# HGRN2 decays by doubling products, and other rotations for a dilated attention, in a two-layer trunk on one core

## The chip, the cores and the metric

The kernel runs on one core of a Trainium2 chip. TensorE (PE) multiplies matrices into PSUM; VectorE (DVE), ScalarE (ACT) and GpSimd (POOL) do the elementwise work, and SyncE (SP) issues every DMA here, in one queue and in order. GpSimd works on SBUF tiles only here. The metric is the time of one execution in microseconds, as the median of several; lower is better.

## The reference

A trunk of two residual layers for 1024 tokens of width 1024, all float32. Layer 0 has a gated DeltaNet and a short convolution as its mixer, layer 1 has HGRN2 and a dilated window attention; a SwiGLU FFN follows each. The change is in layer 1's mixer. What it computes, cut:

```python
hq, hf, hi, hg, sq, sk, sv = split_cols(h @ w_in, CD_SPLITS)
f_gate = lb + (1.0 - lb) * sigmoid(hf)              # 4 heads of 128
k_in   = (1.0 - lb) * sigmoid(-hf)                  # = 1 - f_gate
# HGRN2: S_t = diag(f_t) S_{t-1} + k_t v_t^T,  o_t = S_t^T q_t,  q = silu(hq), v = hi
o_c = rms_norm(o, norm_g) * sigmoid(hg)
# attention: patterns (window, dilation) = (128, 1), (512, 4), (2048, 16), 4 heads of 128 each
sq, sk = rope(sq, pos), rope(sk, pos)
outs, lses = dilated_window_attention(...)          # per pattern, causal
o_d = sum over patterns of outs * softmax(lses over patterns)
return concatenate([o_c, o_d]) @ w_out
```

## The kernel before

Activations are feature-major: 128 features in the partitions, tokens along the row, in two halves of 512 tokens (`HT`). A product in float32 is three matmuls of high and low parts (`mm3`, lines 126 to 128), so a projection of 128 columns for a half is 8 x 3 = 24 matmuls of 512 columns. `wload` (L109) loads a block of weights into a ring (two tiles for raw data, four for the split parts) and splits it with ScalarE (L102) and VectorE (L103). PSUM has 2 banks for `psg`, 3 for `psu`, 3 for `psm`.

Layer 1 before its mixer makes queries, keys, HGRN queries and forget gates in the class `Pairs`: two column blocks at a time, by seven products of half the size, 84 matmuls of 512 columns for a pair where 96 would be plain. `HEADS` lists its sixteen pairs: ("k", p, h) is query and key of pattern p (0, 1, 2 for dilation 1, 4, 16) and head h; ("f", h) is forget gate and query of an HGRN head. The results go to DRAM: `pairs.qk` unrotated, and `pairs.bkq` with b, k and q of a head, where `forget` computes the gate f, its logarithm and a running sum b over 128 tokens by scans.

`mixer_cd` then holds all other work of the mixer. Its outer sequence is dense: value projections of HGRN (`hgrn_v`) and of the three patterns (`swa_v`, in the order 1, 2, 0), then the gates (`hgrn_gates`). Every few matmuls it calls `tick`, which advances two generators by rates: `chain`, the HGRN units, and `local`, the attention with its combine (L2071 to L2080). So the program's text interleaves them; the order on each engine, PE too, is then chosen by the scheduler, by its own estimates.

An HGRN unit is one head and one half, eight in all (`hgrn`). For seven block sizes bs = 1, 2, ..., 64, `decayed` makes a tile m: for every pair of neighbouring blocks it takes b minus its value at the boundary (L1712, L1714), the exponential on ScalarE (L1715), and multiplies by k in the earlier (L1716) and q in the later block (L1720). Products of m with itself in 32x32 blocks on PE (L1728, L1759, L1783) give the masked scores, which are gathered in `attn`. Then k times its decay is transposed (L1790), the states are made (L1798, L1809), and the output of the unit is normalised: sum of squares (L1823, L1824), the power -1/2 `rr` on GpSimd (L1826), a diagonal matrix of it on VectorE (L1828), and a product of the output with that matrix (L1834), which transposes and scales at once.

Attention loads a head's query and key, twice: once as they are and once (`rs`) with the two halves of the features exchanged. GpSimd multiplies these by the tables of sine (L1935) and cosine (L1939), VectorE adds (L1944).

## Time and profile before

| what | us |
| --- | --- |
| three runs | 2648.23, 2653.04, 2654.51; median 2653.04 |
| the profiled execution | 2653.24 |
| its span, the profile's own scale | 2651.4 |
| mean granted clock of TensorE | 0.988 |
| layer 0's mixer | until about 480 |
| layer 0's FFN | 480 to 1141 |
| the pairs | 1141 to 1461 |
| layer 1's mixer | 1461 to 1925 |
| output projection, FFN, final norm | 1925 to 2651 |

The page of the profile gives busy time by engine, the span in 40 slices of 66.3 us, the chain of work that ended last, and groups of instructions by line. Views of the trace give the same by stretch of time (windows), by what an engine waited for (waits), and instruction by instruction (timelines). L1712 means line 1712 of the kernel before. In a row of a group, "x56 | 31.2, 565" is 56 instructions, 31.2 us in all and 565 ns on average, and behind the next bar stands the idle time of the engine ahead of them with what ended it. A stretch where the granted clock is 0.50 has TensorE at half speed.

### The profile page before, as it was taken

The numbers are of one execution on the slowest core, as the hardware profiler recorded it, in microseconds if no ns is written. First come the engines' busy times: TensorE is split into PE (matmuls) and PEld (weight loads), VectorE is DVE, ScalarE is ACT, GpSimd is POOL, SyncE is SP. The second block draws the span as 40 slices with busy tenths as digits, with TensorE's granted clock in tenths as the row PEclk, the third lists the DMA queues.
The fourth block names the chain that finished last, engine by engine and source line by source line (L and its number), as shares of the span: only waits on it lengthen the run. The fifth ranks groups of instructions, "written<-read, shape, count | busy, mean of one in ns | idle before, by whom it ended". The sixth has DMA issues, their size and how long they took to land.

```text
span 2651.4 us, 37677 instructions
## 1 busy us (share of the span) xinstructions
PE 2569.4 (97%) x14163; PEld 2136.8 (81%) x14163; DVE 1731.2 (65%) x2809; ACT 1023.3 (39%) x1719; POOL 677.7 (26%) x552
## 2 busy tenths in 40 slices
PE   8999999999999999999999898998799999999998
PEld 6888888888888888878888777876688888888887
DVE  7887776585655665576665665579767655656554
ACT  4432123343333344434444344444444333334442
POOL 1110111333333200133232313345023433331001
PEclk9999999999999999999999899998999999999999
DMA  4424347325556687623333636876562555658763
GB/s 140 136 97 164 108 146 228 130 86 184 179 201 207 223 295 261 193 88 139 120 122 128 183 124 172 184 208 185 172 228 69 170 171 184 218 198 288 265 192 119
DMA packets 277606, 457.79 MB, mean 173 GB/s; under 512 B 49424, under 2 KB 133936, under 8 KB 276912
## 3 DMA queue, kind: packets, MB, share of 16 engines
q1 hardware_dynamic: 277424, 455.39, 53.6%
q8 instruction: 111, 1.82, 0.3%
q14 instruction: 71, 0.58, 0.1%
HBM read 315.23 MB, written 140.07 MB: 172 GB/s over the span
## 4 chain that ended last, share of the span: by engine, by line
PE 84%; DVE 9%; DMA 3%; issue 2%; POOL 1%; ACT 1%; SPq 0%; DVEq 0%; POOLq 0%; ACTq 0%
PE psu L126 16%; PE psu L127 15%; PE psu L128 15%; PE psg L126 6%; PE psg L128 6%; PE psg L127 6%; PE psm L128 4%; PE psm L126 4%; PE psm L127 4%; DMA raw<-in_dram 1%; DVE h L223 1%; DVE h L592 1%; DMA cm<-scr_o 1%; PE psm L199 1%; DVE w L289 1%
## 5 line engine op out<-in xcount | busy, mean ns | idle before, releaser
L103 DVE TENSOR_TENSOR w<-raw,w 128x1024 fp32r<-128x1024 f32 (+1 forms) x323 | 383.9, 1190 | 158.2 <-ACT w L102 157.6
L102 ACT CAST w<-raw 128x1024 fp32r<-128x1024 f32 (+1 forms) x323 | 309.3, 959 | 287.7 <-PE psu L128 137.6
L126 PE MATMUL psu<-hnh,w 128*128 128x512 f32 x848 | 339.9, 401 | 13.0 <-ACT w L102 7.0
L127 PE MATMUL psu<-hnl,w 128*128 128x512 f32 x848 | 332.9, 393 | 0.8 <-DVE hnl L2186 0.8
L128 PE MATMUL psu<-hnh,w 128*128 128x512 f32 x848 | 332.9, 393 | 0.0
L126 PEld LDWEIGHTS psu<-hnh,w 128*128 128x128 f32 x848 | 161.0, 190 | 46.6 <-ACT w L102 7.0
L302 POOL TENSOR_TENSOR ws<-raw 128x512 f32<-128x512 f32 x54 | 82.0, 1519 | 428.6 <-DMA raw<-in_dram 230.7
L128 PEld LDWEIGHTS psu<-hnh,w 128*128 128x128 f32 x848 | 160.4, 189 | 34.8 <-DVE w L103 0.8
L127 PEld LDWEIGHTS psu<-hnl,w 128*128 128x128 f32 x848 | 160.8, 190 | 33.4 <-DVE hnl L2186 1.3
L187 POOL TENSOR_TENSOR acc<-acc,sq 128x512 f32<-128x512 f32 x48 | 69.9, 1456 | 439.4 <-ACT sq L183 439.4
L103 DVE TENSOR_TENSOR w<-ws,w 128x1024 fp32r<-128x1024 f32 x51 | 65.8, 1290 | 114.0 <-ACT w L102 114.0
L103 DVE TENSOR_TENSOR hidq<-hr,hidq 128x1024 fp32r<-128x1024 f32 x72 | 82.1, 1141 | 73.6 <-ACT hidq L102 73.1
L102 ACT CAST hidq<-hr 128x1024 fp32r<-128x1024 f32 x72 | 70.2, 980 | 100.3 <-DMA hr<-ts 58.1
L308 POOL TENSOR_TENSOR raw<-raw,ws 128x512 f32<-128x512 f32 x51 | 68.0, 1334 | 158.0 <-DVE w L103 156.7
L126 PE MATMUL psm<-hidq,w 128*128 128x512 f32 (+1 forms) x275 | 106.0, 385 | 0.0
L127 PE MATMUL psm<-hidq,w 128*128 128x512 f32 (+1 forms) x275 | 105.8, 385 | 0.0
L128 PE MATMUL psm<-hidq,w 128*128 128x512 f32 (+1 forms) x275 | 105.8, 385 | 0.0
L393 POOL TENSOR_TENSOR hid<-hid,c 128x512 f32<-128x512 f32 x44 | 62.8, 1427 | 125.6 <-ACT hid L392 125.3
L126 PE MATMUL psu<-t4h,w 128*128 128x512 f32 x240 | 93.7, 391 | 0.6 <-ACT c L372 0.6
L127 PE MATMUL psu<-t4l,w 128*128 128x512 f32 x240 | 93.4, 389 | 0.0
L128 PE MATMUL psu<-t4h,w 128*128 128x512 f32 x240 | 93.4, 389 | 0.0
L126 PE MATMUL psu<-t3h,w 128*128 128x512 f32 x240 | 93.4, 389 | 0.0
(491 smaller groups left out, 6774.6 us busy)
## 6 DMA issues: line engine op xcount, KB each, us to landing
raw<-in_dram SPq DMA_DIRECT2D x227, 512.0 KB, 4.0
sd<-in_dram SPq DMA_DIRECT2D x44, 512.0 KB, 3.9
hid<-hid SPq DMA_DIRECT2D x88, 256.0 KB, 2.8
sd<-sd SPq DMA_DIRECT2D x44, 512.0 KB, 3.3
hr<-ts SPq DMA_DIRECT2D x40, 512.0 KB, 4.7
raw<-sd SPq DMA_DIRECT2D x40, 512.0 KB, 4.0
hd<-h SPq DMA_DIRECT2D x48, 256.0 KB, 3.9
h<-hd SPq DMA_DIRECT2D x48, 256.0 KB, 5.6
```

Of the source, the lines that this page charges most:

```text
L102: S.copy(hi, src)
L103: eng.tensor_tensor(lo, src, hi.bitcast(F32), op=SUB)
L126: T.matmul(o, lh, rh, start=first and i == 0, stop=False, **kw)
L127: T.matmul(o, lh, rl, start=False, stop=False, **kw)
L128: T.matmul(o, ll, rh, start=False, stop=last and i == n - 1, **kw)
L187: (eng or G).tensor_tensor(a, a, q, op=ADD)
L199: T.matmul(st[:, j:j + 1], x[:, j * P:(j + 1) * P], onesn, start=i + j == 0, stop=i == 1, skip_group_check=True)
L223: V.scalar_tensor_tensor(h, h, vec[:, row + k:row + k + 1], pb, op0=MULT, op1=MULT)
L289: later(lambda: V.tensor_tensor(u[:, 1, c], src[:, c], u[:, 0, c].bitcast(F32), op=SUB))
L302: G.tensor_tensor(s[:, HT:], b[:, :HT], b[:, HT:], op=ADD)
L308: G.tensor_tensor(a[:, HT:], a[:, HT:], s[:, :HT], op=SUB)
L393: G.tensor_tensor(h, h, self.c22.pop(f), op=MULT)
```

## The change

Decays without logarithms: `forget` stores f itself; the scans and the logarithm go. A unit copies k into kd, and q times f into qd. `level` copies the halves of kd and qd that its products need into m (ScalarE), and then multiplies, in place, kd in the earlier block of each pair by the later block's total decay and qd in the later block by the earlier one's. The totals d of the next level, half as many, are the products of neighbours (`dd`, from 256 down to 4 elements). After the seventh level kd, qd and d are what the states need, so the exponentials at the end go too. f, kk and q have one buffer instead of two. HGRN's values go through DRAM (`scr_h`).

The unit's end: ScalarE sums the squares, the output is scaled from PSUM by `rr` at the start of the next unit (`ending[0]`), and transposed by PE after the next unit's first products (`ending[1]`).

Rotations: pattern 1's queries and keys leave the pairs (`HEADS` has twelve entries) and are plain projections in the mixer (`swa_qk`), rotated by VectorE straight from PSUM. Patterns 2 and 0 are rotated by `turns`, a third generator: 32 items (pattern, head, query or key, half), each loaded, rotated by three GpSimd operations, and stored to DRAM (`final`), from which `Attend` loads it. The combine uses scaled copies on ScalarE and 128x128 multiply-adds on VectorE.

Order: PE follows the text inside `mixer_cd` (`manual_schedule`), the other engines still the scheduler. `tick` advances three generators. At the mixer's end the first three banks of the output projection are begun (`leading`).

```diff
-        HEADS = (("k", 0, 0), ("k", 0, 1), ("k", 0, 2), ("f", 0), ("k", 1, 0), ("k", 1, 1), ("f", 1), ("k", 1, 2),
-                 ("k", 1, 3), ("f", 2), ("k", 2, 0), ("k", 2, 1), ("f", 3), ("k", 2, 2), ("k", 2, 3), ("k", 0, 3))
+        HEADS = (("k", 0, 0), ("k", 0, 1), ("k", 0, 2), ("f", 0), ("k", 2, 0), ("f", 1), ("k", 2, 1), ("f", 2),
+                 ("k", 2, 2), ("f", 3), ("k", 2, 3), ("k", 0, 3))
 
...
-            for c, r in zip(cs, rs):
-                S.activation(r, c, AF.Ln, scale=self.omlb[:, h:h + 1], bias=self.lb[:, h:h + 1])
-            yield
-            for half, (c, r) in enumerate(zip(cs, rs)):
-                for j in range(4):
-                    t = slice(j * P, (j + 1) * P)
-                    V.tensor_tensor_scan(c[:, t], onec[:, 0:1].to_broadcast([P, P]), r[:, t], 0.0, op0=MULT, op1=ADD)
+                S.activation(c, c, AF.Identity, scale=om, bias=lb)
                 dma(self.bkq[h, half][0], c)
                 yield
 
...
-                    raws[u] = [hl(n, bufs=2) for n in ("b", "kk", "q")]
+                    raws[u] = [hl(n) for n in ("f", "kk", "q")]
...
-            def hgrn(h, half, states):
...
-                    m = hl("m", bufs=3)
-                    mb = v4(m)
-                    ref = bb[:, :, 0, bs - 1:bs].to_broadcast([P, n, bs])
-                    V.tensor_tensor(mb[:, :, 1, :], bb[:, :, 1, :], ref, op=SUB)
-                    if bs > 1:
-                        V.tensor_tensor(mb[:, :, 0, :], ref, bb[:, :, 0, :], op=SUB)
-                        S.activation(m, m, AF.Exp)
-                        V.tensor_tensor(mb[:, :, 0, :], mb[:, :, 0, :], kb[:, :, 0, :], op=MULT)
-                    else:
-                        S.activation(mb[:, :, 1, :], mb[:, :, 1, :], AF.Exp)
-                        S.copy(mb[:, :, 0, :], kb[:, :, 0, :])
-                    V.tensor_tensor(mb[:, :, 1, :], mb[:, :, 1, :], qb[:, :, 1, :], op=MULT)
...
+            def level(bs, k, q, d, dd, at):
+
+                n = HT // (2 * bs)
+
+                def v4(ap):
+                    return ap.rearrange("p (n a j) -> p n a j", a=2, j=bs)
+                m, kb, qb, d3 = hl("m", bufs=4), v4(k), v4(q), d.rearrange("p (n a) -> p n a", a=2)
+                S.copy(v4(m)[:, :, 0, :], kb[:, :, 0, :])
+                S.copy(v4(m)[:, :, 1, :], qb[:, :, 1, :])
+                for x, i in ((kb, 0), (qb, 1)):
+                    V.tensor_tensor(x[:, :, i, :], x[:, :, i, :], d3[:, :, 1 - i:2 - i].to_broadcast([P, n, bs]), op=MULT)
+                nd = dd[:, at:at + n]
+                V.tensor_tensor(nd, d3[:, :, 0], d3[:, :, 1], op=MULT)
+                return m, nd, at + n
...
+            def hgrn(u, states, ending):
+                h, half = divmod(u, 2)
+                f, kk, q = raws.pop(u)
+                kd, qd, dd = hl("kd"), hl("qd", bufs=2), hl("dd")
+                state = [f, 0]
+
+                def next_level(bs):
+                    m, state[0], state[1] = level(bs, kd, qd, state[0], dd, state[1])
                     return m
...
-                ms = [decayed(1), decayed(2)]
+                ending[0]()
+                S.copy(kd, kk)
+                V.tensor_tensor(qd, q, f, op=MULT)
+                ms = [next_level(1), next_level(2)]
+                yield
+                ms.append(next_level(4))
+                yield
+                od = psg()
+                blocks(od[:, 0:P], kk, q)
+                for i in range(3):
+                    blocks(od[:, (i + 1) * P:(i + 2) * P], ms[i], ms[i])
+                ending[1]()
+                ac = hl("ac", (4, 32))
+                V.tensor_tensor(ac, c4(od[:, 0:P]), dia32[:, None, :].to_broadcast([P, 4, 32]), op=MULT)
+                for i in range(3):
+                    take(i, od[:, (i + 1) * P:(i + 2) * P])
+                ask(u + 1)
+                ms = [next_level(8), next_level(16)]
...
+                oq, ss, rr = hl("e4", (4, P), 3), hl("ss", (4,), 2), hl("rr", (4,), 2)
+                for c in range(4):
+                    S.activation(oq[:, c, :], po[:, c * P:(c + 1) * P], AF.Square, accum_out=ss[:, c:c + 1])
+                V.tensor_scalar(ss, ss, 1.0 / P, 4 * EPS, op0=MULT, op1=ADD)
+                with tc.high_priority(offset=300):
+                    G.tensor_tensor(rr, ss, mhalf[:, 0:4], op=ALU.pow)
...
+                def scaled():
+                    V.tensor_tensor(os_, c4(po), rr[:, :, None].to_broadcast([P, 4, P]), op=MULT)
+
+                def end():
+                    o = psg()
+                    for c in range(4):
+                        T.transpose(o[:, c * P:(c + 1) * P], os_[:, c, :], ident)
+                    go = hl("e4", (4, P), 3)
+                    S.activation(go, c4(o), AF.Copy, scale=hgg)
+                    dma(scr_g[half, h].rearrange("p (c t) -> p c t", c=4), go)
+                    done_c[0] = u + 1
                 yield
...
-                    T.matmul(o[:, c * P:(c + 1) * P], os_[:, c, :], dg[:, c, :], start=True, stop=True)
-                go = hl("e4", (4, P), 3)
-                V.tensor_scalar(go, c4(o), vec[:, R_HGG:R_HGG + 1], 0.5, op0=MULT, op1=MULT)
...
+            def leading(tick):
...
+                ws[2] = wload(("cdo", 2), ("cdo", 3))
+                for d, bank in ((0, psg), (1, psg), (2, psu)):
+                    o = banks[d] = bank()
+                    for ks in ((0, 1), (2, 3), (4, 5)):
+                        proj(wk(ws[d // 2 * 2], d % 2), qs, ks, o, first=ks[0] == 0, last=False)
+                        tick(0.5)
...
+            turn12 = tl("turn12", (2, 320))
+            dma(turn12, c_rope[:, :, T_LEN:])
+            final = {(p, h): dr.tile([2, P, 2, HT], F32, name=f"fin{p}{h}") for p in (2, 0) for h in range(4)}
...
+            def swa_qk(h, tick):
+
+                w = wload(("cd", 20 + h), ("cd", 32 + h))
+                qk = [tl("q", (2, HT), 2), tl("k", (2, HT), 2)]
+                for half in range(NH):
+                    for i, z in enumerate(qk):
+                        o = proj(wk(w, i), hn[half], range(KH), last=False)
+                        tick(1)
+                        proj(wk(w, i), hn[half], range(KH, KT), o, first=False)
+                        x = tl("sw", bufs=2)
+                        S.copy(x[0:64], o[64:128])
+                        S.copy(x[64:128], o[0:64])
+                        o3, x3 = (y.rearrange("p (i r) -> p i r", r=4) for y in (o, x))
+                        for y, t in ((x3, 1), (o3, 0)):
+                            V.tensor_tensor(y, y, turn12[:, t, half * P:(half + 1) * P, None].to_broadcast([P, P, 4]), op=MULT)
+                        V.tensor_tensor(z[:, half].rearrange("p (r i) -> p i r", r=4), o3, x3, op=ADD)
+                        tick(1)
+                return qk
+
...
+            def turns():
+
+                items = [(2, h, i, half) for h in range(4) for i in range(2) for half in range(NH)]
+                items += [(0, h, i, half) for half in range(NH) for h in range(4) for i in range(2)]
+                held, table, out = {}, {}, []
+
+                def ask_c(n):
+                    if n < len(items):
+                        p, h, i, half = items[n]
+                        held[n] = c, x = tl("tc", bufs=2), tl("tx", bufs=2)
+                        src = pairs.qk[p, h][i, :, half]
+                        dma(c, src)
+                        dma(x[0:64], src[64:128])
+                        dma(x[64:128], src[0:64])
+                ask_c(0)
+                for n, (p, h, i, half) in enumerate(items):
+                    if p == 0 and half not in table:
+                        table[half] = tl("turn0", (2, HT))
+                        dma(table[half], c_rope[:, :, half * HT:(half + 1) * HT])
+                        yield
+                    c, x = held.pop(n)
+                    ask_c(n + 1)
+                    for y, t in ((x, 1), (c, 0)):
+                        if p == 0:
+                            G.tensor_tensor(y, y, table[half][:, t], op=MULT)
+                        else:
+                            y3 = y.rearrange("p (r i) -> p r i", r=16)
+                            at = 256 + half * 32
+                            G.tensor_tensor(y3, y3, turn12[:, t, None, at:at + 32].to_broadcast([P, 16, 32]), op=MULT)
+                    G.tensor_tensor(c, c, x, op=ADD)
+                    yield
+                    dma(final[p, h][i, :, half], c)
+                    turned.add((p, h, i, half))
...
-            due, rate = [0.0, 0.0], [0.0, 4 / 3]
+            hg_chain, loc, turner = chain(), local(), turns()
+            works = (loc, hg_chain, turner)
+            due, rate = [0.0] * 3, [0.0, 0.7, 0.5]
...
-            hgrn_v(0, pairs.first, lambda cost: None, range(0, 4))
-            have_v[0] = 1
-            hgrn_v(0, pairs.first, tick, range(4, 8))
-            for p in (1, 2, 0):
-                swa_v(p, tick)
-                ready += [(h, p) for h in range(4)]
-                rate[0] = 1.4 if p == 0 else 0.8
-                if p == 2:
-                    hgrn_v(1, wload(("cd", 10), ("cd", 11)), tick)
-                    have_v[0] = 2
-            hgrn_gates(tick)
-            while ready or busy[0]:
-                next(loc)
+            E = mybir.EngineType
+            with tc.manual_schedule(engines={E.PE}):
+                hgrn_v(0, pairs.first, lambda cost: None, range(0, 4))
+                have_v[0] = 1
+                hgrn_v(0, pairs.first, tick, range(4, 8))
+                swa_v(1, tick)
+                query_keys((0, 1))
+                hgrn_v(1, wload(("cd", 10), ("cd", 11)), tick)
+                have_v[0] = 2
+                query_keys((2, 3))
+                for p in (2, 0):
+                    swa_v(p, tick)
+                    ready += [(h, p, None) for h in range(4)]
+                    rate[0] = 1.0
+                ws = [wload(("cd", 12 + 2 * i), ("cd", 13 + 2 * i)) for i in range(2)]
+                for half in range(NH):
+                    hgrn_gates(half, ws, tick)
+                leading(tick)
+                while ready or busy[0]:
+                    next(loc)
```

The scheduler's order of PE for the first unit's levels, before (psg and psu are PSUM tiles, m a level's tile; the rows of L126 to L128 are dense):

```order
L1728 MATMUL psg<-q,kk 32x32 x16
L1728 MATMUL psg<-m 32x32 x32
L126 MATMUL psu<-w,t1h 128x256
L127 MATMUL psu<-w,t1h 128x256
...
L1728 MATMUL psg<-m 32x32 x32
L126 MATMUL psu<-w,hnh 128x512
L127 MATMUL psu<-w,hnh 128x512
L1728 MATMUL psg<-m 32x32 x16
L128 MATMUL psu<-w,hnl 128x512
```

and of the change, at the same place:

```order
L1723 MATMUL psg<-q,kk 32x32 x16
L1723 MATMUL psg<-m 32x32 x48
L126 MATMUL psu<-w,hnh 128x512
L127 MATMUL psu<-w,hnh 128x512
L128 MATMUL psu<-w,hnl 128x512
...
L1767 MATMUL psg<-cf,kd 128x128 x4
L1723 MATMUL psg<-m 32x32 x32
L1773 MATMUL psg<-m 32x32 x8
L1778 MATMUL psg<-m 64x64 x4
L126 MATMUL psu<-w,hnh 128x512
```

The first block of products now holds three levels instead of two. Where 24 dense rows of 256 columns and then two of 512 stood between a unit's groups of products, 54 rows of 512 columns now stand between the first three levels and the last four, and the transposes of kd come ahead of these.

GpSimd around the first units' `rr`, before (rs, q and k are the tiles being rotated):

```order
L1939 TENSOR_TENSOR q<-q,rope 128x512 x2
L1935 TENSOR_TENSOR rs<-rs,rope 128x512 x2
L1939 TENSOR_TENSOR k<-k,rope 128x512 x2
L1935 TENSOR_TENSOR rs<-rs,rope 128x512 x2
L1826 TENSOR_TENSOR rr<-ss,mhalf 128x4
L1935 TENSOR_TENSOR rs<-rs,rope 128x512 x4
L1826 TENSOR_TENSOR rr<-ss,mhalf 128x4 x2
```

and of the change (tc and tx are an item's two tiles):

```order
L1948 TENSOR_TENSOR tc<-tc,tx 128x512
L1947 TENSOR_TENSOR tx<-tx,turn_11051 128x512
L1947 TENSOR_TENSOR tc<-tc,turn_11051 128x512
L1948 TENSOR_TENSOR tc<-tc,tx 128x512
L1821 TENSOR_TENSOR rr<-ss,mhalf 128x4
L1947 TENSOR_TENSOR tx<-tx,turn_11051 128x512
L1947 TENSOR_TENSOR tc<-tc,turn_11051 128x512
L1948 TENSOR_TENSOR tc<-tc,tx 128x512
```

The first `rr` stood behind 16 rotations, the second and third behind 20. Now the first stands behind 30, ten items, the second behind 17 items, the third behind 26, and the other five behind all 32.

296 lines of the change are left out of this document (124 added, 172 removed).

## The prediction

> **What bounds the kernel now.** The page comes first:
>
> ```profile
> span 2651.4 us, 37677 instructions
> PE 2569.4 (97%) x14163; PEld 2136.8 (81%) x14163; DVE 1731.2 (65%) x2809; ACT 1023.3 (39%) x1719; POOL 677.7 (26%) x552
> PE   8999999999999999999999898998799999999998
> PEclk9999999999999999999999899998999999999999
> PE 84%; DVE 9%; DMA 3%; issue 2%; POOL 1%; ACT 1%; SPq 0%; DVEq 0%; POOLq 0%; ACTq 0%
> ```
>
> TensorE (PE) sets the time. It is below nine tenths at the two ends and in slices 23, 25, 28 and 29 of 66.3 us (1458 to 1525, 1591 to 1657, 1790 to 1922); the granted clock falls in two of these. That is the second layer's mixer, where the edit is. Next the windows view by stage: columns are start:end, length, busy time of PE, weight load, VectorE (DVE), ScalarE (ACT) and GpSimd (POOL) with instructions, then granted clock, DMA share and GB/s.
>
> ```profile
> 60.00:480.00 420.00, 418.79 (x2422) 352.70 (x2422) 307.85 (x675) 122.34 (x289) 53.45 (x104) 1.00 0.46 148
> 1200.00:1440.00 240.00, 240.00 (x1061) 198.71 (x1060) 151.68 (x153) 101.69 (x138) 79.01 (x52) 1.00 0.34 122
> 1461.00:1925.00 464.00, 405.11 (x3924) 340.23 (x3923) 326.45 (x838) 199.48 (x515) 147.93 (x107) 0.94 0.65 177
> 1461.00:1700.00 239.00, 216.93 (x2083) 186.63 (x2081) 141.41 (x324) 98.34 (x239) 75.73 (x59) 0.95 0.65 171
> 1700.00:1925.00 225.00, 188.18 (x1843) 153.60 (x1842) 185.05 (x514) 101.14 (x276) 72.20 (x49) 0.93 0.66 184
> ```
>
> The pair products (second row) run without a hole: 1061 products of 512 columns in 240 us, 0.2262 us each. The mixer (third row) leaves PE idle for 464 - 405.11 = 58.9 us: 22.1 before 1700 (239 - 216.93), 36.8 after. The first row is the other layer's mixer, whose PE order is written by hand: 1.2 us idle. Third, the stretches in which the granted clock is 0.50; there are seven, their first row and sum being
>
> ```profile
> 1495.53:1509.18 13.65, 5.45 (x73) 3.96 (x74) 13.65 (x17) 4.43 (x8) 11.33 (x8) 0.50 0.27 75
> sum 54.57, PE 35.10 PEld 29.18 DVE 44.02 ACT 24.12 POOL 21.57; mean PE 5.01 PEld 4.17 DVE 6.29 ACT 3.45 POOL 3.08
> ```
>
> so half of the 35.1 busy, 17.5 us, is lost to the clock. Fourth, PE's waits from 1461 to 1925 (us, times, longest), which say where the idle time comes from:
>
> ```profile
> PE psg L1728 <- DVE m L1720: 13.6, 5, 6.9
> PE psu L2085 <- DVE ol L2080: 11.7, 5, 7.1
> PE psg L1834 <- DVE e L1828: 8.0, 6, 3.8
> PE psu L126 <- ACT hnh L102: 6.0, 2, 4.8
> ```
>
> HGRN levels, the combine, the head's normalisation and a weight split that is late: nearly all are VectorE. Why it is late where it is only 70% busy, the timelines of VectorE and GpSimd show:
>
> ```profile
> 1468.56 0.42 DVE L1712 TENSOR_TENSOR m<-b 128x256 f32<-128x256 f32 x1
> 1492.06 1.48 DVE L1712 TENSOR_TENSOR m<-b 128x256 f32<-128x256 f32 x1
> 1487.28 2.53 POOL L1935 TENSOR_TENSOR rs<-rs,rope 128x512 f32<-128x512 f32 x2
> 1493.22 2.85 POOL L1935 TENSOR_TENSOR rs<-rs,rope 128x512 f32<-128x512 f32 x2
> ```
>
> The same VectorE operation takes 0.42 us with GpSimd idle and 1.48 while GpSimd rotates; the two GpSimd operations take 2.85, 1.42 each, instead of 2.53.
>
> **The change, part by part**, against the profiled execution's own 2653.2 us (0.2 from the median, 2653.04).
>
> *Matmuls.* Four pair products go (4 x 84), four heads' dense products come (4 x 96): 48 more of 512 columns, x 0.2262 = +10.9. The pair stage has no idle PE and sheds VectorE work, so it shortens by its whole 336 x 0.2262 = 76 us and the mixer grows by 86.9.
>
> *The head's output.* Eight full fp32 products with a diagonal become transposes:
>
> ```profile
> 1514.78 0.45 PE psg L1790 x4
> 1525.69 1.16 PE psg L1834 x8
> ```
>
> A transposed head takes 0.45 (first row), the diagonal one 1.16: -0.71 x 8 units = -5.7.
>
> *Decays.* Each level loses its subtractions and exponentials:
>
> ```profile
> L1712 DVE TENSOR_TENSOR m<-b 128x256 f32<-128x256 f32 x56 | 31.2, 565 | 10.4 <-PE psg L1728 9.4 <-PE psg L1783 0.8
> L1714 DVE TENSOR_TENSOR m<-b 128x256 f32<-128x256 f32 x48 | 26.1, 544 | 0.0
> L1944 DVE TENSOR_TENSOR q<-q,rs 128x1024 f32<-128x1024 f32 x12 | 19.6, 1634 | 29.9 <-POOL rs L1935 17.1 <-POOL q L1939 12.8
> L1944 DVE TENSOR_TENSOR k<-k,rs 128x1024 f32<-128x1024 f32 x12 | 15.7, 1310 | 11.5 <-POOL rs L1935 4.6 <-POOL k L1939 4.1 <-DMA rs<-qk 2.7
> L798 DVE TENSOR_TENSOR fc<-gt,psm 128x512 f32<-128x512 f32 x4 | 2.7, 683 | 1.4 <-issue 1.4
> L798 DVE TENSOR_TENSOR d<-gt,psm 128x512 f32<-128x512 f32 x9 | 9.4, 1048 | 8.8 <-PE psm L128 4.8 <-issue 4.0
> ```
>
> VectorE loses 57.3 of subtractions and the rotations' 35.3 of additions. The dense heads' rotation, four heads x 2 operands x 2 halves = 16 times two products from PSUM (0.68 each by the last row but one) and a strided sum (1.05, last row), gives 39 back. Each 2.4 lies beside 24 matmuls, 5.4 us, and three banks turn over; uncovered it would cost those 39. Still two multiplies with both inputs in SBUF are left at each of seven levels, with the query's one and seven small ones: 22 a unit.
>
> *Smaller edits, taken at nothing together.*
>
> ```profile
> L1715 ACT ACTIVATE m<-m 128x512 f32<-128x512 f32 x48 | 30.1, 630 | 45.5 <-DVE m L1714 44.5 <-DVE dn L2073 0.7
> L1719 ACT COPY m<-kk 128x256 f32<-128x256 f32 x8 | 3.4, 428 | 4.3 <-PE psg L1728 4.0 <-DMA kk<-bkq 0.2
> ```
>
> ScalarE makes two copies of 0.43 a level, 112 in all or 48 us, for the exponentials' 30 and the copies' 3.4: 15 more on an engine that is busy 199 of 464. PE's other work hides it; uncovered it costs 15. The gate, query and key tiles of a unit lose their second buffer, so the next unit's three loads are issued only when the present unit's first four products are out. They then have some 84 dense products (19 us) for a landing of about 5. The value tiles gain a store and a load through DRAM (2.4 and 4.6 below), issued long before. The output projection's 54 products that move ahead of its own stage cost PE the same there; what they fill, the 6.0 of late split, is in the 58.9 already. The combine has fewer full-width passes on VectorE.
>
> *Rotations.* GpSimd has 96 operations before and after:
>
> ```profile
> L1935 POOL TENSOR_TENSOR rs<-rs,rope 128x512 f32<-128x512 f32 x48 | 68.4, 1446 | 69.1 <-DMA rs<-qk 44.0 <-DVE cm L2077 7.5 <-DVE ol L2046 6.4
> rs<-qk SPq DMA_DIRECT2D x48, 256.0 KB, 4.6
> scr_g<-e SPq DMA_DIRECT2D x8, 256.0 KB, 2.4
> 1523.90 1.03 POOL rr L1826
> 1524.95 0.70 DVE e L1828
> ```
>
> but 32 items of three now run as one stream from the mixer's start. An item needs at least 3 x 1.42 = 4.3 us. A buffer's round is a load of 4.6, two operations on it, 2.8, and a store of 2.4, 9.8 for two buffers, so 4.9 an item, which I take; load and store end to end, 7.0, are the upper bound. The stream lasts 32 x 4.9 = 157 us and lies under the first three to four units. The head's rr (1.03) goes through GpSimd as well, and stands in its order behind ten items for the first unit: ready 50 us after the stream's start. PE wants its transposes after 54 + 84 dense products (31 us) and, an estimate, 14 for the small ones and the attention set-up, about 45: 5 us late. Behind a late rr stand, on VectorE, the scaling and the next unit's multiplies; PE waits for these.
>
> *PE's order.* Written by hand, it puts 48 to 54 dense products (11 to 12 us) between a unit's early levels and its late ones, where before some 24 short ones stood. So the whole 58.9 of idle and the 17.5 of slow clock fall away first, and new ones come in. Bounds for the new idle: 1.2 x 464/420, about 1, and the old 58.9. While the stream runs I take 28: 5 for the first rr, 2 attention, 9 and 12 for the transposes of units 2 and 3, whose multiplies (15 of SBUF, up to 1.48 instead of 0.42) come after a held rr. The part of before nearest to it agrees: 22.1 idle in 239 us with 75.7 of GpSimd, so 40 by 96 x 1.42 = 136 of it. After the stream GpSimd is idle and VectorE at 0.42: 9, a quarter of the 36.8. With 10 for the clock (four stretches of 17.5/7 = 2.5) it is 47.
>
> Sum: 2653.2 + 10.9 - 5.7 - 58.9 - 17.5 + 47 = 2629.
>
> The seven slow stretches last 3.4 to 13.7 us and stand at the long holes. The Trainium skill ("TensorE: Matmul & The Clock Gate", Part 1: The HAM clock gate) puts the drop to half after an idle window of about 3.4 us; the trace's lengths, multiples of 3.41, agree. By that rule waits each shorter would leave the clock whole, and the sum would be 2619.
>
> **The rivals.**
>
> *All hidden* (0.22). The hand order covers each wait, as in the first layer's 418.79 of 420: 2 idle, rr and clock 10: 2653.2 + 10.9 - 5.7 - 58.9 - 17.5 = 2582, + 12 = 2594. For it speaks VectorE's load, less by 57.3 + 35.3 - 39 = 54; against it that no GpSimd stream of 157 us lies in that stage (53.45 busy of 420).
>
> *GpSimd holds VectorE* (0.18), the other side.
>
> ```profile
> L1720 DVE TENSOR_TENSOR m<-m,q 128x256 f32<-128x256 f32 x56 | 29.4, 524 | 1.7 <-ACT m L1718 1.6
> L1716 DVE TENSOR_TENSOR m<-m,kk 128x256 f32<-128x256 f32 x48 | 25.6, 532 | 2.2 <-ACT m L1715 2.2
> L2080 DVE TENSOR_TENSOR ol<-ol,cm 128x512 f32<-128x512 f32 x16 | 16.1, 1005 | 0.0
> L2077 DVE TENSOR_TENSOR cm<-cm,w 128x512 f32<-128x512 f32 x16 | 14.6, 952 | 0.0
> ```
>
> All 22 multiplies of a unit wait for a whole GpSimd operation: 22 x 1.42 = 31, 13 for the dense rotations (39/3), and 18 for attention, splits and the rest (326.45 less the levels' 112.3, the rotations' 35.3 and the combine's 30.7, over eight) make 62 us a unit; PE has 402 dense products x 0.2262 = 91 and about 11 a unit beside them in three units, 125. 186 - 125 = 61 late, with 9 for rr, 15 later and 15 clock: 100, so 2682. It decides from a new idle of 71 (2653.2 - 2582), units of about 54 us. For it: 1.48 of 0.42 above. Against it: over the whole mixer the mean is 0.565 with GpSimd busy for a third of it, and 0.42 + 1.06 x 0.32 would be 0.76 if every overlap cost the full wait. The Trainium skill ("SBUF — State Buffer", Who interferes with whom) states an exclusive port that is held for a whole instruction, the second to issue blocking until the first ends; the rows agree with it (1.48, about one GpSimd operation), and by it alone, at every multiply, this rival would be the outcome.
>
> *Queue* (0.15). SP takes its DMAs in order, and the query and key weights stand behind stores that wait for GpSimd. One such late weight cost 4.8 (the fourth wait). Four heads: 4 x 5 = 20, so 2649, no change. Against it stands a ring of four weight buffers, loaded early.
>
> **How the numbers follow.** Forecast 0.45 (its own range 2607 to 2660, idle 25 to 78), all hidden 0.22, GpSimd 0.18, queue 0.15. A measurement here tells 0.3%, 8 us: faster is below 2645, slower above 2661. Faster: 0.22 + 0.38 of the forecast + 0.03 of the queue = 0.63; slower: 0.16 + 0.02 + 0.01 = 0.19; 0.18 between. The range is 2590 (all hidden with almost nothing left) to 2670 (part of the GpSimd case).
>
> **What would show it.** Pair stage 76 us shorter, still without idle time. The diagonal products gone, with the transposes waiting for the scaling behind rr in the first units and hardly later. Mean of the level multiply: near 0.42 (hidden), 0.6 to 0.9 (forecast), about 1.4 (GpSimd). 96 GpSimd rotations in one stream of 136 to 224 us. The mixer's idle plus clock loss at 47; below 20 or above 71 breaks the forecast, and so does an idle stretch before a query or key product that waits for its weights, or any change above 5 us in the stages outside.

## The result and the profile after

The change takes 2626.71 us (median; 2622.28 to 2629.71) beside 2653.78 for the kernel before on the same chip, a ratio of 0.9896 (95% interval 0.9871 to 0.9922). That is 27 us faster; 2629 was forecast. The profiled execution took 2629.71, its span is 2627.9. The page, in the rows shown of the kernel before:

```profile
span 2627.9 us, 37803 instructions
PE 2564.8 (98%) x14179; PEld 2138.1 (81%) x14179; DVE 1656.1 (63%) x2718; ACT 1032.6 (39%) x1855; POOL 643.5 (24%) x536
PE   8999999999999999999999879999999999999998
PEclk9999999999999999999999989999999999999999
PE 79%; DVE 9%; DMA 4%; issue 3%; ACT 2%; POOL 2%; SPq 1%; POOLq 0%; DVEq 0%; ACTq 0%
```

PE is below nine tenths in two slices of the mixer (the 23rd and 24th, 1445 to 1577) where before there were four. The windows by stage, in the columns of the prediction, cut at the first value product and at the second half's FFN norm, which both kernels have. Before, the pairs and the mixer with the output projection:

```profile
1141.00:1461.90 320.90, 317.66 (x1413) 262.77 (x1412) 216.38 (x226) 138.39 (x184) 101.15 (x63) 1.00 0.34 119
1461.90:1975.30 513.40, 454.51 (x4149) 381.41 (x4148) 356.40 (x870) 220.66 (x544) 159.46 (x115) 0.95 0.67 186
```

and after:

```profile
1140.00:1391.80 251.80, 243.96 (x1078) 200.75 (x1077) 176.11 (x166) 104.76 (x145) 76.96 (x47) 0.99 0.33 117
1391.80:1951.70 559.90, 523.71 (x4501) 444.67 (x4500) 318.24 (x840) 263.88 (x719) 152.21 (x115) 0.97 0.65 197
```

The pairs lose 69.1 us, the mixer gains 46.5, the work ahead of the pairs ends 1.0 earlier, and what follows is the same to 0.1: -23.6 of the two spans' -23.5. Idle time of PE in the mixer goes from 58.9 to 36.2 (559.90 - 523.71). The pairs are no longer without holes: 251.80 - 243.96 = 7.8, against 3.2. The stretches at half clock, one of 6.83 us left out here but not in the sum; the first lies in the pairs, the others in the mixer:

```profile
1165.65:1169.06 3.41, 3.41 (x10) 2.76 (x10) 3.07 (x5) 0.00 (x0) 0.24 (x1) 0.50 0.00 0
1448.96:1459.20 10.24, 5.46 (x20) 5.01 (x21) 6.41 (x12) 6.70 (x25) 7.55 (x7) 0.50 0.89 275
1554.77:1568.42 13.65, 4.69 (x20) 4.51 (x21) 6.10 (x10) 1.58 (x5) 9.71 (x9) 0.50 0.70 188
1629.86:1633.28 3.42, 3.42 (x10) 2.68 (x9) 0.64 (x4) 0.99 (x4) 0.00 (x0) 0.50 0.36 135
...
1896.10:1899.52 3.42, 3.42 (x10) 2.68 (x11) 2.38 (x7) 1.43 (x4) 0.00 (x0) 0.50 0.34 128
sum 40.97, PE 26.28 PEld 22.98 DVE 23.50 ACT 15.18 POOL 17.51; mean PE 4.38 PEld 3.83 DVE 3.92 ACT 2.53 POOL 2.92
```

Without the first, half of 22.9 is 11.4 us. Idle and slow clock together are 47.6 where they were 58.9 + 17.5 = 76.4. PE's waits there (us, times, longest):

```profile
PE psm L2014 <- DVE k L1915: 14.4, 2, 12.2
PE psg L1811 <- ACT attn L1791: 7.4, 2, 6.8
PE psm L2061 <- DVE pt L2063: 3.3, 1, 3.3
PE psm L2061 <- ACT sc L2021: 2.5, 3, 2.0
PE psu L2134 <- DVE ol L2127: 2.2, 1, 2.2
```

The waits for level tiles and for the diagonal are gone, and that for a late weight split is down to 1.1 us. Two long ones are new: 12.2 us for pattern 1's rotated keys (L1915) and 6.8 for HGRN's scores (L1791). VectorE's timeline ahead of the first, with GpSimd rotating most of the time (idle time and its releaser in brackets):

```profile
1530.46 1.45 DVE L1914 TENSOR_TENSOR sw<-sw,turn 128x512 f32<-128x512 f32 x1 [0.32 <-ACT sw L1911]
1531.83 0.69 DVE L1914 TENSOR_TENSOR psu<-psu,turn 128x512 f32<-128x512 f32 x1
...
1548.13 0.41 DVE L1713 TENSOR_TENSOR kd<-kd,dd 128x256 f32<-128x256 f32 x1
1548.46 2.54 DVE L1715 TENSOR_TENSOR dd<-dd 128x16 f32<-128x16 f32 x2
...
1552.05 1.48 DVE L1713 TENSOR_TENSOR qd<-qd,dd 128x256 f32<-128x256 f32 x1
...
1558.22 0.69 DVE L1825 TENSOR_TENSOR e<-psg,rr 128x512 f32<-128x512 f32 x1 [3.47 <-POOL rr L1821]
...
1562.65 1.03 DVE L1915 TENSOR_TENSOR k<-psu,sw 128x512 f32<-128x512 f32 x1
```

The level multiply takes 0.41 us in a pause of GpSimd and 1.48 beside one of its operations; then VectorE stands 3.47 us before the scaling because rr is behind an item; the rotation of the keys comes last. The second wait has another source. ScalarE's and SP's timelines:

```profile
1448.73 0.58 ACT L1884 COPY sw<-psu 128x512 f32<-128x512 f32 x1 [9.09 <-DMA scr_v<-sw]
```

```profile
1438.00 0.32 SPq L1930 DMA_DIRECT2D tc<-qk  x1
1441.02 0.32 SPq L1950 DMA_DIRECT2D fin<-tc  x1
...
1443.73 0.38 SPq L1885 DMA_DIRECT2D scr_v<-sw  x1
```

ScalarE waits 9.09 us for a buffer of the value rows, whose store stands in SP's order behind the store of an item (L1950) that waits for GpSimd: 4.1 us pass until that store is issued, and 5.0 more until its buffer is free. The copies of the scores stand behind it on ScalarE. In the pairs 5.6 of the 7.8 us of holes have one line, four times, with its cause in ScalarE's timeline:

```profile
PE psu L126 <- ACT u L365: 5.6, 4, 1.6
```

```profile
1268.38 0.81 ACT L832 ACTIVATE fc<-fc,lb,omlb 128x512 f32<-128x512 f32 x1 [6.26 <-DVE kk L830]
1269.10 0.56 ACT L365 COPY u<-psu 128x512 f32<-128x512 f32 x1
```

`forget`'s new last step waits on ScalarE for VectorE's reciprocal, and a copy that PE needs is behind it.

### The profile page after: what moved, and what is told of

Read it like the earlier page. It is cut to its first block, busy times and chain, and to the rows that moved or that the text cites. A ratio compares the mean times of both kernels' runs of the same rounds, so it can differ in the third digit from the quotient of the medians.

```text
span 2627.9 us, 37803 instructions
## 1 busy us (share of the span) xinstructions
PE 2564.8 (98%) x14179; PEld 2138.1 (81%) x14179; DVE 1656.1 (63%) x2718; ACT 1032.6 (39%) x1855; POOL 643.5 (24%) x536
## 4 chain that ended last, share of the span: by engine, by line
PE 79%; DVE 9%; DMA 4%; issue 3%; ACT 2%; POOL 2%; SPq 1%; POOLq 0%; DVEq 0%; ACTq 0%
PE psu L126 15%; PE psu L128 15%; PE psu L127 15%; PE psg L126 5%; PE psg L128 5%; PE psg L127 5%; PE psm L127 4%; PE psm L128 4%; PE psm L126 4%; DMA tc<-qk 1%; DVE fc L828 1%; DMA cm<-scr_o 1%; PE psm L2072 1%; DVE h L223 1%; DMA raw<-in_dram 1%
## 5 line engine op out<-in xcount | busy, mean ns | idle before, releaser
L126 PE MATMUL psu<-hnh,w 128*128 128x512 f32 x888 | 356.8, 402 | 8.0 <-ACT w L102 8.0
L127 PE MATMUL psu<-hnl,w 128*128 128x512 f32 x888 | 349.1, 393 | 0.2 <-DVE hnl L2250 0.2
L128 PE MATMUL psu<-hnh,w 128*128 128x512 f32 x888 | 349.1, 393 | 0.0
L126 PEld LDWEIGHTS psu<-hnh,w 128*128 128x128 f32 x888 | 168.5, 190 | 42.2 <-ACT w L102 8.4
L128 PEld LDWEIGHTS psu<-hnh,w 128*128 128x128 f32 x888 | 168.3, 190 | 36.4 <-DVE w L103 0.8
L127 PEld LDWEIGHTS psu<-hnl,w 128*128 128x128 f32 x888 | 168.6, 190 | 34.2 <-DVE hnl L2250 0.8
L187 POOL TENSOR_TENSOR acc<-acc,sq 128x512 f32<-128x512 f32 x48 | 69.7, 1452 | 511.4 <-ACT sq L183 507.3
L302 POOL TENSOR_TENSOR ws<-raw 128x512 f32<-128x512 f32 x50 | 73.6, 1473 | 422.2 <-DMA raw<-in_dram 295.2
L126 PE MATMUL psm<-hidq,w 128*128 128x512 f32 (+1 forms) x275 | 106.1, 386 | 0.0
L128 PE MATMUL psm<-hidq,w 128*128 128x512 f32 (+1 forms) x275 | 105.9, 385 | 0.0
L126 PE MATMUL psu<-t3h,w 128*128 128x512 f32 x224 | 87.7, 392 | 5.6 <-ACT u L365 5.6
L308 POOL TENSOR_TENSOR raw<-raw,ws 128x512 f32<-128x512 f32 x47 | 61.3, 1304 | 121.0 <-DVE w L103 119.8
L126 PE MATMUL psu<-t4h,w 128*128 128x512 f32 x224 | 87.6, 391 | 0.6 <-ACT c L372 0.5
L127 PE MATMUL psu<-t3l,w 128*128 128x512 f32 x224 | 87.3, 390 | 0.0
L127 PE MATMUL psu<-t4l,w 128*128 128x512 f32 x224 | 87.3, 390 | 0.0
```

Source lines behind the costliest of these rows:

```text
L126: T.matmul(o, lh, rh, start=first and i == 0, stop=False, **kw)
L127: T.matmul(o, lh, rl, start=False, stop=False, **kw)
L128: T.matmul(o, ll, rh, start=False, stop=last and i == n - 1, **kw)
L187: (eng or G).tensor_tensor(a, a, q, op=ADD)
L302: G.tensor_tensor(s[:, HT:], b[:, :HT], b[:, HT:], op=ADD)
L308: G.tensor_tensor(a[:, HT:], a[:, HT:], s[:, :HT], op=SUB)
```

## The experiments

Each experiment was timed beside runs of the kernel before on its own chip: 2652.48 for experiments 1 to 4, 2649.61 for 5, 6, 8 and 9, 2653.28 for 7 and 10 to 12. So kernels are compared by their differences from it; the change itself stands at -27.1 (2626.71 - 2653.78).

The theory at first was the prediction's: PE's hand order takes the old idle time away, and the GpSimd stream brings new. The rival: VectorE's lighter work took it away, and the order does not matter.

**1. The scheduler's order.**

```diff
-            with tc.manual_schedule(engines={E.PE}):
+            with ExitStack():
                 hgrn_v(0, pairs.first, lambda cost: None, range(0, 4))
```

> The change with TensorE's order in the second mixer left to the scheduler again, all else as it is. Theory (the hand order removes the 58.9 us of idle and 17.5 of slow clock that the scheduler's order had, and what is idle now, 36.2 with 11.4 of slow clock in the mixer and the output projection, comes from the GpSimd stream): idle and slow clock go back to about 76, so 2627 + 29 = 2656, range 2645 to 2670. Rival (VectorE's lighter work removed them, the order does not matter): within 8 us of the change, 2619 to 2635.

Measured: 2619.61, ratio 0.9875 (0.9856 to 0.9894), -32.9. The window of its mixer:

```profile
1390.90:1938.10 547.20, 520.81 (x4502) 442.67 (x4501) 314.82 (x840) 264.74 (x719) 152.22 (x115) 0.97 0.67 201
```

PE is idle for 26.4 us where the change has 36.2, at the same clock; the old 76 do not come back. The interval overlaps the change's, so the order written by hand gains nothing that can be told. The prediction's step on PE's order is wrong here, and the rival is left.

**2. No turns.** Attention loads patterns 2 and 0 from where the pairs left them.

```diff
-                        while not all((p, h, i, half) in turned for i in range(2) for half in range(NH)):
-                            next(turner)
-                        dma(self.k, final[p, h][1])
+                        dma(self.k, pairs.qk[p, h][1])
...
+                for n in range(32):
+                    yield
+                    yield
```

> The change without its stream of turns: patterns 2 and 0 use queries and keys unrotated, straight from where the pairs left them; no GpSimd rotation, none of their loads and stores. Theory (the stream brings nearly all of the 36 us of idle and 11 of slow clock that are left): 33 to 42 us faster than the change, 2585 to 2594, level multiplies at 0.42. Rival (the fixed order itself waits for results that come late anyway): less than 12 us faster, 2615 to 2627.

Measured: 2594.73, ratio 0.978 (0.9765 to 0.9795), -57.8: 31 us less than the change. The windows view of its mixer, and a group of its level multiplies:

```profile
1391.20:1916.80 525.60, 514.78 (x4502) 437.92 (x4501) 272.23 (x840) 263.89 (x719) 19.28 (x19) 0.99 0.54 160
L1713 DVE TENSOR_TENSOR kd<-kd,dd 128x256 f32<-128x256 f32 x48 | 20.3, 423 | 6.9 <-ACT m L1710 5.1
```

Idle time is 10.8 instead of 36.2. Most of what is left idle in the change is the stream's doing, as forecast, though 31 is 2 us less than the 33 to 42 expected.

**3. GpSimd alone** and **4. the queue alone** split it. In experiment 3 GpSimd works on private tiles without any transfer, in an order written by hand; in experiment 4 the turns are loaded and stored without being rotated. In both, attention has patterns 2 and 0 unrotated.

```diff
+                c, x = tl("tc"), tl("tx")
...
+                for n in range(32):
+                    for y, t in ((x, 1), (c, 0)):
+                        y3 = y.rearrange("p (r i) -> p r i", r=16)
+                        G.tensor_tensor(y3, y3, turn12[:, t, None, 256:288].to_broadcast([P, 16, 32]), op=MULT)
+                    G.tensor_tensor(c, c, x, op=ADD)
+                    if n % 3:
+                        yield
...
-            with tc.manual_schedule(engines={E.PE}):
+            with tc.manual_schedule(engines={E.PE, E.Pool}):
```

> As the run without turns, but GpSimd does 96 multiplications and sums of 128x512 on tiles of its own, ordered among the units' powers about as in the change (before the first 24 to 27, the second 40, the third 67, the fourth 88); no loads, no stores; patterns 2 and 0 unrotated. Theory that VectorE held by GpSimd is the larger part: level multiplies at 1.0 to 1.3 during the stream, 15 to 25 us slower than without turns, 2605 to 2615. Rival (SP's queue is the larger part): within 8 us of the run without turns, though the multiplies are as slow.

```diff
                     ask_c(n + 1)
-                    for y, t in ((x, 1), (c, 0)):
...
-                    G.tensor_tensor(c, c, x, op=ADD)
                     yield
                     dma(final[p, h][i, :, half], c)
```

> The change with the loads and stores of its turns but without GpSimd's 96 operations (the loaded tiles are stored as they are, so patterns 2 and 0 are unrotated). SP then waits for landings where it waited for GpSimd. Theory that GpSimd's hold on VectorE is the larger part: level multiplies at 0.42 and 20 to 30 us faster than the change, 2597 to 2607. Rival (SP's queue): less than 12 us faster, with ScalarE's value copies still waiting for their stores, 2615 to 2627.

Measured: GpSimd alone 2618.16, ratio 0.9873 (0.9857 to 0.989), which is 23.4 above the run without turns; the queue alone 2606.43, ratio 0.9828 (0.9797 to 0.986, some 8 us to either side), 11.7 above it. Together 35, and the change is 31 above. The windows of the two mixers, with a group of level multiplies of each; GpSimd alone:

```profile
1392.60:1939.90 547.30, 518.79 (x4501) 439.19 (x4500) 323.06 (x842) 264.08 (x719) 157.53 (x115) 0.98 0.51 153
L1713 DVE TENSOR_TENSOR qd<-qd,dd 128x256 f32<-128x256 f32 x48 | 34.0, 708 | 0.1
```

and the queue alone:

```profile
1390.50:1927.10 536.60, 518.34 (x4502) 439.50 (x4501) 271.95 (x840) 263.23 (x719) 19.26 (x19) 0.99 0.68 205
L1713 DVE TENSOR_TENSOR kd<-kd,dd 128x256 f32<-128x256 f32 x48 | 20.3, 423 | 5.9 <-ACT m L1710 4.1
```

Idle 28.5 and 18.3 beside 10.8. GpSimd's hold on VectorE is about twice the queue's share, which is known less well. Experiment 3 does not delay rr as it was meant to: its stream starts only behind the first rr, at 1452, and VectorE waits 8.1 us for rr in all, as without turns (8.3), where the change has 13.2. So the 23 us are VectorE's slower products without a late rr. The stream is also stretched over 209 us where the change has 185 (1411 to 1596), and the 60 multiplies in it have a mean of 0.86, below the 1.0 to 1.3 expected; over the whole mixer the mean is close to the change's. Of the times expected, 2605 to 2615 was missed by 3 us; 2597 to 2607 was met, but with each chip's own kernel before as the measure the queue alone is 19 us faster than the change, not 20 to 30.

**5. The hand order on the kernel before.**

```diff
+            with tc.manual_schedule(engines={mybir.EngineType.PE}):
+                hgrn_v(0, pairs.first, lambda cost: None, range(0, 4))
...
+                hgrn_gates(tick)
```

> The kernel before with TensorE's order in the second mixer as the program's text has it, nothing else of the change. The change kept its time with the scheduler's order (2620 beside 2627), so the theory now is that lighter VectorE work removed the idle time and the order did nothing: no gain here, 2645 to 2680, TensorE waiting for the level tiles. Rival (the hand order is worth something where VectorE is heavier): 2635 or less.

Measured: 2688.48, ratio 1.0146 (1.0131 to 1.0161): 39 us slower. PE's waits:

```profile
PE psg L1728 <- DVE m L1720: 23.0, 7, 7.8
PE psg L1798 <- ACT e L1791: 18.1, 5, 8.0
```

In the old text's order PE waits longer for the level tiles than in the scheduler's (13.6). Writing PE's order by hand, taken alone, is a loss, 8 us beyond the range expected. The old text was not laid out for it, so this is no measure of what the order does in the change; experiments 1, 6 and 7 are.

**6. The old decays in the change.** `level` is replaced by `decayed`, the gate by its logarithm and scans, and the exponentials at the unit's end come back.

```diff
-                raws[u] = [hl(n) for n in ("f", "kk", "q")]
+                raws[u] = [hl(n, bufs=2) for n in ("b", "kk", "q")]
-                ms = [next_level(1), next_level(2)]
+                ms = [decayed(1), decayed(2)]
...
+                S.activation(t, b, AF.Exp)
+                V.tensor_tensor(q, q, t, op=MULT)
```

> The change with the decays of before (logarithm and scans in the pairs; two subtractions, an exponential and two multiplications a level; exponentials at the unit's end), all else as in the change, f, kk and q in two buffers. Theory (the doubling products removed most of the 76 us of idle and slow clock): 25 to 50 us slower than the change, 2650 to 2677. Rival (rotations that are done ahead of time and the later end of a unit removed them): within 10 us, 2617 to 2637.

Measured: 2653.93, ratio 1.0012 (1.0003 to 1.0022), +4.3: the whole gain is gone, 31 us. Its mixer and two of the four groups of level operations:

```profile
1386.40:1978.10 591.70, 534.65 (x4501) 451.86 (x4500) 369.79 (x915) 267.88 (x683) 156.42 (x115) 0.95 0.62 188
L1729 DVE TENSOR_TENSOR m<-b 128x256 f32<-128x256 f32 x56 | 37.7, 680 | 22.5 <-PE psg L1714 19.8 <-DMA b<-bkq 2.6
L1731 DVE TENSOR_TENSOR m<-b 128x256 f32<-128x256 f32 x48 | 33.8, 705 | 0.0
```

Idle time is 57.1 where the change has 36.2, and the mixer is 31.8 us longer; the pairs, without the new last step of `forget`, end 5.4 earlier. The two subtractions a level, 71.5 us, are back, as slow under the stream as any other, and VectorE is busy 51.6 us more. PE's longest waits:

```profile
PE psm L2072 <- ACT sc L2032: 10.1, 2, 9.3
PE psu L126 <- ACT sw L1895: 8.1, 1, 8.1
```

The first is for the attention's scores, the second for value rows. No wait for a level tile stands in the list, in experiment 7 neither.

**7. The old decays and the scheduler's order**, experiments 1 and 6 together.

> The change with the decays of before and with TensorE's order left to the scheduler: the fourth corner beside the change (2627), the scheduler's order alone (2620) and the old decays alone (2654). Theory (the decays are worth it whatever the order): 2640 to 2656. Rival (only a fixed order makes the old decays dear): 2630 or less.

Measured: 2649.74, ratio 0.9985 (0.9975 to 0.9995), -3.5. Beside experiment 1 the decays are worth 29 us, beside the change 31: the same under either order. The window of its mixer:

```profile
1386.40:1974.90 588.50, 534.51 (x4502) 451.42 (x4502) 371.36 (x915) 267.06 (x683) 154.37 (x115) 0.95 0.62 188
```

54.0 idle, at a mean clock of 0.95, as before. So all other parts of the change together gain 3.5 us under the scheduler's order and lose 4.3 under the hand order, and the rival is shown: without the lighter decays the idle time stays.

**8. Pattern 1 in the pairs again**, rotated by the stream.

```diff
+        HEADS = (("k", 0, 0), ("k", 0, 1), ("k", 0, 2), ("f", 0), ("k", 1, 0), ("k", 1, 1), ("f", 1), ("k", 1, 2),
...
-            due, rate = [0.0] * 3, [0.0, 0.7, 0.5]
+            due, rate = [0.0] * 3, [0.0, 1.07, 1.1]
-                query_keys((0, 1))
+                ready += [(h, 1, None) for h in range(4)]
```

> The change with pattern 1's queries and keys in the pairs again (16 pairs) and rotated by the stream of turns, now 48 items and 144 GpSimd operations; the generators' rates are raised to 1.07 and 1.1 because 32 of 92 ticks go with the dense products. By the terms so far: 48 matmuls fewer, -10.9; half as much again of GpSimd's 23 us and of the queue's 12 (the runs without turns, with GpSimd alone and with the queue alone), +17: 2633, range 2622 to 2645. Rival (dense products are what PE does while units wait): 2650 or more.

Measured: 2695.19, ratio 1.0171 (1.0156 to 1.0186), +45.6, some 60 us above what was expected. One row of PE's waits, and ScalarE's timeline, say where:

```profile
PE psu L126 <- ACT w L102: 52.1, 2, 32.3
```

```profile
1592.52 0.58 ACT L1884 COPY sw<-psu 128x512 f32<-128x512 f32 x1 [22.30 <-DMA scr_v<-sw]
1603.87 1.04 ACT L102 CAST w<-raw 128x1024 fp32r<-128x1024 f32 x1 [10.77 <-DMA raw<-in_dram]
```

A store of value rows stands behind several items in SP's order, the next weights stand behind that store, and PE waits 32 us for them; a second such wait makes 52. This is the rival "Queue" of the prediction at full size. The run does not tell what the dense products are worth, since its items also come twice as fast, and 52 us of its waits are these two.

**9. rr on ScalarE**, as exp(-ln/2).

```diff
-                with tc.high_priority(offset=300):
-                    G.tensor_tensor(rr, ss, mhalf[:, 0:4], op=ALU.pow)
+                S.activation(rr, ss, AF.Ln)
+                S.activation(rr, rr, AF.Exp, scale=-0.5)
```

> The change with rr computed by ScalarE as exp(-ln/2) instead of GpSimd's power, so that it no longer stands behind turns. Theory (rr behind turns is part of GpSimd's 23 us: 7.8 us of VectorE's waits in the first units): 3 to 8 us faster, 2619 to 2624. Rival (the hold on VectorE's multiplies is all, or ScalarE's table changes cost as much): within 3 us or slower.

Measured: 2622.66, ratio 0.9897 (0.9882 to 0.9912), -27.0, which is the change's own ratio. The time lies in the range expected only because this chip's kernel before is 4 us faster too. The 3.47 us before rr is a wait that others take the place of: PE still waits 10.2 us for pattern 1's keys (14.4 in the change), and 6.7 for an HGRN state.

**10. No lead.** The output projection's 54 early products go back to its own stage (`leading` is not called, and `out_proj` gets nothing ready).

> The change without the 54 products of the output projection that are made at the mixer's end; they are made in its own stage instead. Taken at nothing in the prediction: 2624 to 2630. Rival (they fill the waits of the last attention and combine): 5 to 12 us slower, with TensorE waiting before the output projection.

Measured: 2630.32, ratio 0.9916 (0.9897 to 0.9934), -23.0. That is 4 us behind the change, with intervals that overlap: unclear. PE's wait for the combine (`ol`) is 5.6 us where the change has 2.2.

**11. Three mends** of what the profile after showed: the scheduler's order, rr on ScalarE, and `forget`'s last step on VectorE.

```diff
-                S.activation(c, c, AF.Identity, scale=om, bias=lb)
+                V.tensor_scalar(c, c, om, lb, op0=MULT, op1=ADD)
```

> The change with three mends: TensorE's order left to the scheduler (-7), rr on ScalarE (-4), and the gate's last step in the pairs on VectorE instead of ScalarE, where it waits for the reciprocal and holds up a copy that four of the pairs need (-5.6). If they add up: 2610, range 2604 to 2616, no idle time in the pairs. If the first two lie on each other: 2614 to 2620.

Measured: 2608.42, ratio 0.9836 (0.9817 to 0.9855), -44.9: faster than both kernels, by 18 us than the change. Pairs and mixer:

```profile
1140.00:1383.00 243.00, 240.55 (x1072) 198.86 (x1071) 179.31 (x173) 98.51 (x136) 76.50 (x47) 1.00 0.35 122
1383.00:1929.70 546.70, 524.12 (x4501) 445.35 (x4500) 309.42 (x839) 286.83 (x751) 143.89 (x107) 0.97 0.67 201
```

The pairs are 8.8 us shorter, of which 5.4 were idle (7.8 less 2.4) and 1.7 the slow stretch that this run did not have. The mixer is 13.2 shorter, with 22.6 idle. The total is as forecast (2610), but rr gained nothing by itself (9), so the parts are not those that were summed.

**12. Late stores** on top of these: an item's store is issued one item later, from three buffers.

```diff
-                    dma(final[p, h][i, :, half], c)
-                    turned.add((p, h, i, half))
+                    out.append((c, p, h, i, half))
+                    if len(out) > 1:
+                        store()
```

> The three mends and, besides, the store of an item issued one item later, with three buffers for it, so that SP waits less for GpSimd. Theory (the queue's 12 us are SP's waits for the item just rotated): 4 to 10 us faster than the three mends. Rival (the scheduler has set the stores late enough, or the waits move to the loads): within 3 us of them.

Measured: 2609.23, ratio 0.9838 (0.9819 to 0.9858): the same. SP's wait for GpSimd only moved from the store (47.9 us up to 1625) to the load of the item's other tile (35.4, L1931 in that kernel), which still has two buffers. A third buffer for that one was not tried.

## Why the prediction was right, and where not

The time was right to 2 us, the sum's last term too, and yet one step gave the gain to the wrong part.

- **What bounds it**: right. The change plays in the mixer, and what it leaves unchanged behind it is the same to 0.1 us.
- **Matmuls**, +10.9: the pairs' work fell by 75.4 at full clock (317.66 to 243.96 less 1.7), 76 expected. The stage fell by 69.1, because its four forget heads now make PE wait 1.4 us each, and 1.7 more is the slow stretch. The prediction looked at VectorE there, which has room, and not at ScalarE's order.
- **The head's output**, -5.7, and the rest of PE's work: the mixer's work grew by 75.3 (523.71 - 11.4 against 454.51 - 17.5) where 81.2 was summed. Where the 6 us come from, no run takes apart.
- **PE's order**: here the prediction failed, "So the whole 58.9 of idle and the 17.5 of slow clock fall away first". With the old decays the hand order leaves 57.1 of idle (experiment 6), leaving it out of the change costs nothing (1), and by itself it costs the kernel before 39 us (5). What takes the old idle away is the next item.
- **Decays**: costed at nothing on the path, they are the gain, 29 to 31 us (6 and 7). A level had four VectorE operations on SBUF tiles and an exponential between them; it has two and a small one, and the tile PE needs is a copy of what is there already. The prediction saw that VectorE loses 57.3 us, and says of PE's waits that "nearly all are VectorE", but did not price the one by the other. How the relief reaches PE is not shown in detail: with the old decays in the new text PE does not wait for level tiles but for the attention's scores, value rows and states, which VectorE and ScalarE make as well. Nor is it shown which part of the decays counts, since the subtractions, the exponentials and the steps at a unit's end were only changed together.
- **The new idle and clock**, 47: measured 47.6, of which idle 36.2 (37 forecast) and clock 11.4 (10). Its causes are the stream's: without it 14.2 are left (10.8 idle, 3.4 clock), GpSimd's hold adds 23 and the queue 12 by their times, which is 49. Its places were not those named: pattern 1's keys (14.4) and HGRN's scores behind a store (7.4), not the transposes of kd (9 and 12). That the total agrees is thus partly luck, since 28 of it were a guess at places, and the row that the prediction calls in agreement with the 28 gives 40.
- **The level multiply**: 0.6 to 0.9 us was forecast; its two big groups have means of 0.704 and 0.697:

```profile
L1713 DVE TENSOR_TENSOR kd<-kd,dd 128x256 f32<-128x256 f32 x48 | 33.8, 704 | 4.6 <-ACT m L1710 2.5 <-ACT e L1818 0.5
L1713 DVE TENSOR_TENSOR qd<-qd,dd 128x256 f32<-128x256 f32 x48 | 33.5, 697 | 0.3
```

- **All hidden**, 2594: the run without turns is at 2594.73. That is what the change would give if its rotations cost nothing. Its terms were 12 (2 idle, 10 for rr and clock); measured are 14.2, most of it idle.
- **GpSimd holds VectorE**, 2682: the mechanism is there, 23 us of it, but not at every multiply: with 0.42 alone and 1.2 to 1.5 beside GpSimd, a mean of 0.70 is about one in three, because the stream ends when about half of the units are through: 50 of the 112 lie in its 185 us (157 forecast, 136 to 224 the bounds) and have a mean of 0.99.
- **Queue**, 2649: the mechanism is there too. The queue costs 12 us, and not through weights; through weights it showed in experiment 8, at 52. The wait behind value rows (6.8) takes GpSimd's delay as well: with the queue alone PE's wait for the scores' copies is 0.7. Which waits make up the 12 is open.
- **The clock**: the rule of the Trainium skill ("TensorE: Matmul & The Clock Gate", Part 1: The HAM clock gate) would have given 2619 with waits below 3.4 us each. Two waits were longer (12.2 and 6.8) and have the two long stretches. But the short ones did not leave the clock whole: 1629.86 and 1896.10 start after waits of 2.2 us (14.4 - 12.2, and L2134), and the stretch left out above, 6.83 us, at one of 3.3. The measurement decides, and a gap of 2.2 us can cost 1.7.

What stays open is what pattern 1's dense products gain by themselves, what the early products of the output projection do, and which of VectorE's and ScalarE's old steps PE was waiting for in the end.

## What to carry to other kernels

When a profile says that the bounding engine waits for another, price the other engine's relief too, before giving the gain to a new order: here 51.6 us less of VectorE's work were worth some 30, and the fixed order, with a text laid out for it, changed where the waits are and not the time. The waits on the list need not be the ones that matter, since others can take their place. A stream of work on an engine off the path still costs through what it shares: here what slows VectorE's products beside GpSimd's, about two thirds, and an in-order DMA queue, about one third. And in such a queue a DMA that must wait for a slow engine should not stand ahead of one that a fast engine waits for; a third buffer for one of an item's two tiles did not help that.

## What the runs showed of the hardware

A VectorE product of two SBUF tiles that meets a GpSimd operation here took about as long as that operation, from the largest level product down to the smallest: 1.48 us for 128x256 in the timeline above, and 2.54 for two of the smallest together, the first of 128x16. Without turns (experiment 2) they take 0.42 and 0.17 each; GpSimd's own rotations have means of 1.34 to 1.54. With one operand in PSUM the time is the same as without GpSimd: 0.69 for the 128x512 product right behind one from SBUF that took 1.45. Over all sixteen of each the means are 0.690 from PSUM, where it is 0.693 without turns, and 0.878 from SBUF, where it is 0.692. The Trainium skill ("SBUF — State Buffer", Who interferes with whom) states the lock for two SBUF inputs, and the rows agree. That a product of a few columns pays as much as one of 256 columns, several times its own length, was not expected here.
